# Attention: products of probabilities and values paired on TensorE's two column halves

## The chip, the cores and the metric

One core of one Trainium2 chip runs the whole layer. The metric is the device time of one execution in microseconds (us), the median of several runs. TensorE multiplies matrices (its weight loads are listed apart, as PEld), VectorE (DVE), ScalarE (ACT) and GpSimd (POOL) do the elementwise work, and SyncE (SP) issues the loads of the weights.

## The reference, cut to what matters

The layer is an encoder layer over 512 tokens of width 1024: a recurrent mixer and a windowed attention side by side, merged by gates, then a gated convolution network. Everything is float32. The change touches the attention alone. It has 8 query heads in two groups of four; the heads of a group share one head of keys and values (64 wide). The tokens are cut into four blocks of 128, and a query sees the keys of its own block and of the neighbours on either side, within 128 tokens:

```python
scores = jnp.einsum('bnqhgd,bnkhd->bnhgqk', qb, kb).astype(jnp.float32) * (hd ** -0.5)
...
probs = jax.nn.softmax(jnp.concatenate([scores, sink_logit], axis=-1), axis=-1)[..., :-1]
out = jnp.einsum('bnhgqk,bnkhd->bnqhgd', probs.astype(v.dtype), vb)
```

The last line is the product of probabilities and values. The first and the last block of queries see two blocks of keys, the two in the middle three, so there are ten pairs of a query block and a key block, for each of the two groups.

## The kernel before, in words

**The work around the attention.** Projections of the modulated input come first (`proj_tm`, `proj_fm`, names `tm` and `fm` in the profile). Each is a generator that yields after three matmuls with an estimate of their time. A class `Stream` holds a list of such projections, the background. `drive` (line 411) runs a foreground generator, and each number that the foreground yields is a time that is then filled with steps of the background. Thus the order of TensorE's instructions is laid out by the numbers `A0` to `A5` and their like (lines 34 to 51). An instruction that is passed through `kp` stays behind the instruction that was traced before it on its engine; others may be placed earlier by the scheduler, which works out the order of every engine from its own estimate of durations. When the background is used up, the branch product of the recurrent heads (`branch`, name `yr`, 96 matmuls) and the projections of the attention's gate (`use_ga`, line 956, name `fm` again, evicted by ScalarE at line 959) come after the attention in the program, and the scheduler puts them into the places where TensorE would wait.

**The attention** (from line 771). Eight units, one for each query block `tb` and group `kv`, in the order of `units`. `attention` (line 898) goes over them: in step `i` it runs `scores` of unit `i` and `values` of unit `i - 1` in turn, one step of either. Before the first group's unit of a block come `turn_k` and `turn_q`, which turn keys and queries (names `pk`, `pq`).

`scores` (line 814) multiplies for each of the four heads (name `as`), VectorE takes the product out of its bank with the running maximum (line 826), and after the fourth head come the statistics (lines 830 to 832 on VectorE), the exponentials (line 834 on ScalarE) and the normalization (line 840 on VectorE).

`values` (line 843) takes the normalized probabilities `s` of a unit. For each block of keys `b`, TensorE transposes four pieces of 128 x 128 (name `pt`, line 858), ScalarE evicts them into a tile `pT` of 128 x 512 (line 861), and after the next yield the inner function `product` (line 851) multiplies the block before with the values `v_att` (name `ao`, line 852). The product is float32, 64 rows of result by 512 columns, and goes to one half of the bank `outs[tb]`: to partitions 0 to 63 for the first group (`kv` 0), to 64 to 127 for the second, which is also the half of the array's columns that it uses. When the second group is done, ScalarE copies the bank into `o_att` (line 869).

**Banks and rings.** PSUM has three rings: `mm` (three banks, projections and branches), `sc` (two, transposes of probabilities and others) and `at` (three: scores, turned keys and queries, and the result `outs`). The tile `pT` has a ring of four. The recurrent scan uses the same way of halves as the change: `half_products` (line 595) multiplies float32 tiles of 64 columns in turn on the one and the other half of the array (names `pl`, `pd`, line 600).

Of the kernel before, what the change touches and what calls it, by code (L numbers as in the profile page):

```python
# [8 lines left out]
F32 = mybir.dt.float32  # L9
# [7 lines left out]
P = 128  # L17
# [6 lines left out]
HD = 64  # L24
# [7 lines left out]
C_AQ, C_AK, C_GR, C_GA = 2560, 3072, 3328, 4352  # L32
# schedule parameters
LEAD = 13600
# [10 lines left out]
A2 = 100  # L45
# [5 lines left out]
DVE0 = 6  # L51
# end of schedule parameters
TWO_PI = 6.283185307179586
# [8 lines left out]
def encoder_layer(  # L62
# [28 lines left out]

# [1 line left out]
    def w_tile():  # L93
# [21 lines left out]

# [1 line left out]
    ident = cn.tile([P, P], F32, name="ident")  # L117
# [6 lines left out]
    with tc.tile_pool(name="st", bufs=1) as st:  # L124
# [84 lines left out]

        # the first piece's last terms come from TensorE itself, which has nothing else to do yet  # L210
        first_pm = [sc_ps("pm0_0"), at_ps("pm0_1")]
# [107 lines left out]

# [1 line left out]
    # Each is a generator: TensorE's order is fixed, and what waits for other engines (scans, attention)  # L321
    # is placed between steps of projections that are ready.
    def load_cols(*cols):
# [29 lines left out]
    def proj_tm(use):  # L353
        def steps(parts):
            for b in range(2):
                acc = mm_ps(f"tm{b}")
                for i in range(2):
                    t = slice((2 * b + i) * P, (2 * b + i + 1) * P)
                    for k in range(KT):
                        hi, lo = parts[k // 4]  # L360
                        o = (k % 4) * 256
                        mm3(acc[:, i * 256:(i + 1) * 256], u_hi[:, k, t], u_lo[:, k, t], hi[:, o:o + 256],
                            lo[:, o:o + 256], k == 0, k == KT - 1, kp)
                        if i == 1 and k == KT - 1:
                            use(b, acc.rearrange("p (i n) -> p i n", i=2))
                        yield 327
        return steps
# [46 lines left out]

# [1 line left out]
    def ada_steps(col, done):  # L416
# [64 lines left out]

# [1 line left out]
    lbv = cols_a[:, 17:33].rearrange("p (d l h) -> p d l h", d=2, l=2)  # L483
# [23 lines left out]
    with tc.tile_pool(name="mx", bufs=1) as mx:  # L507
# [87 lines left out]
        def half_products(dst, keys, queries, other=0):  # L595
            # per block of 128: tokens of either half as keys, against the same half (or the other) as queries
            for cc in range(NTB):
                for a in range(2):
                    k_, q_ = cc * P + 64 * a, cc * P + 64 * (a ^ other)
                    kp(nc.tensor.matmul(dst[64 * a:64 * a + 64, q_:q_ + 64], lhsT=keys[:, k_:k_ + 64],  # L600
                                        rhs=queries[:, q_:q_ + 64], start=True, stop=True,
                                        tile_position=(0, 64 * a)))

        def scan_head(h, need):
# [21 lines left out]
            while L <= 128:  # L626
# [32 lines left out]
                L *= 2  # L659
            # across the blocks of 128: a running state per direction, the sum over past tokens of decayed k times v  # L660
            ktok = []
# [43 lines left out]
        def use_v(hh):  # L705
            return lambda b, a: nc.scalar.copy(v_rec[:, 2 * b:2 * b + 2, 256 * hh:256 * hh + 256], a)
# [18 lines left out]
        ri_load = lambda: ri_parts  # L725
        bg.add(ri_load, proj_tm(use_v(0)))                                                  # 1
        bg.add(load_cols(C_AK), proj_tm(use_kv))                                  # 2
        bg.add(load_cols(C_AQ), proj_tm(use_q(0)))                                # 3
        bg.add(load_cols(C_AQ + 256), proj_tm(use_q(1)))                          # 4
        for h in (2, 3):  # L730
            bg.add(load_cols(C_RFF + h * P, C_RFB + h * P), proj_fm(lambda f, a, h=h: gate_f(f, h, a)))
            bg.add(load_half(C_RQ + h * P), proj_fm(lambda f, a, h=h: silu_q(h, a), nf=1))
            if h == 2:
                bg.add(load_cols(C_RI + 256), proj_tm(use_v(1)))                  # 5 6 7, 8 9
        for hh in range(2):
            bg.add(load_cols(C_RG + 256 * hh), proj_tm(use_rg(hh)), ada_hook)               # 10 11
        gr_a = yin.tile([P, 2, S], F32, name="gr_a")
# [31 lines left out]

# [1 line left out]
        with tc.tile_pool(name="at", bufs=2) as at:  # L771
            units = [(tb, kv) for tb in range(NTB) for kv in range(2)]
            span = lambda tb: (max(tb - 1, 0), min(tb + 1, NTB - 1))
            probs, outs = {}, {}
            # scores of float32 accuracy in two passes: [hi; lo] of q on 128 rows against [hi; hi] and [lo; lo] of k
            kT = at.tile([P, 2, 2, S], F32R, name="kT", bufs=1)
# [65 lines left out]

            def values(tb, kv):
                lo_b, hi_b = span(tb)
                rw = slice(kv * HD, kv * HD + HD)
                s = probs.pop((tb, kv))
                if kv == 0:
                    outs[tb] = at_ps(f"ao{tb}")
                po = outs[tb]

                def product(b, pT):
                    kp(nc.tensor.matmul(po[rw, :], lhsT=v_att[:, b, rw], rhs=pT, start=(b == lo_b),
                                        stop=(b == hi_b), tile_position=(0, kv * HD)))
                last = None
                for b in range(lo_b, hi_b + 1):
                    pt = sc_ps(f"pt{tb}_{kv}_{b}")
                    for g in range(NG):
                        kp(nc.tensor.transpose(pt[:, g * P:(g + 1) * P],
                                               s[:, g, (b - lo_b) * P:(b - lo_b + 1) * P], ident))
                    pT = at.tile([P, 512], F32, tag="pT", name="pT", bufs=4)  # L860
                    nc.scalar.copy(pT, pt)
                    yield A2
                    if last is not None:
                        product(*last)
                    last = (b, pT)
                yield A2
                product(*last)
                if kv == 1:
                    nc.scalar.copy(o_att[:, :, tb * P:(tb + 1) * P], po.rearrange("p (g t) -> p g t", t=P))

# [3 lines left out]
            def rec_norm():  # L874
                # RMS norm and output gate of the recurrent heads
                nc.vector.tensor_scalar(rstat, rstat, 1.0 / P, RMS_EPS, ALU.mult, ALU.add)
                nc.scalar.activation(rstat, rstat, AF.Sqrt)
                nc.vector.reciprocal(rstat, rstat)
                for h in range(NH):
                    for tb in range(NTB):  # L880
                        nc.vector.scalar_tensor_tensor(out=o_tok[:, tb, h], in0=o_tok[:, tb, h],
                                                       scalar=rstat[:, tb, h:h + 1],
                                                       in1=rgs[:, tb, h * P:(h + 1) * P], op0=ALU.mult, op1=ALU.mult)
# [39 lines left out]

# [1 line left out]

# [27 lines left out]
    with tc.tile_pool(name="br", bufs=1) as br:  # L953
# [9 lines left out]
        def early_out():  # L963
            # the first two row blocks of w_out, into space that the recurrent branch has left
            hi = big.tile([P, 2, D], F32R, tag="x0", name="wo_hi")
            lo = big.tile([P, 2, D], F32R, tag="x1", name="wo_lo")
            raw = w_tile()
            rv = raw.rearrange("p (k n) -> p k n", n=D)
            nc.sync.dma_start(rv, w_out[0:2 * P, :].rearrange("(k p) n -> p k n", p=P))
            for k in range(2):  # L970
                nc.scalar.copy(hi[:, k], rv[:, k])
                nc.vector.tensor_tensor(out=lo[:, k], in0=rv[:, k], in1=hi[:, k].bitcast(F32), op=ALU.subtract)
                wo.append((hi[:, k], lo[:, k]))
# [48 lines left out]

# [1 line left out]
    u2p = ctx.enter_context(tc.tile_pool(name="u2p", bufs=1))  # L1024
# [129 lines left out]

# [1 line left out]
    ff = ctx.enter_context(tc.tile_pool(name="ff", bufs=2))  # L1156
# [37 lines left out]

# [1 line left out]
    vt = u2p.tile([P, 2, D], F32, tag="ua", name="vt")  # L1196
# [35 lines left out]
    for j in range(2):  # L1232
# [16 lines left out]
        for tb in range(NTB - j):  # L1249
# [3 lines left out]
            if j == 1:  # L1253
                mv = layer_stats(ff, bst2[:, tb, 0:2], f"b{tb}")
                for h in range(2):
                    scaled(tb, mv, 512 * h, 512 * h + 512)
                    store(tb, 512 * h, 512 * h + 512)
    # the last block ends in quarters
    tb = NTB - 1
# [37 lines left out]
```

## Time and profile before

| | |
|---|---|
| median of 3 runs | 826.77 us (825.41 to 827.01) |
| profiled execution, span from the first to the last instruction | 827.1 us; nothing of its time is recorded outside the span |
| TensorE matmuls busy | 803.9 us, 97% |
| VectorE busy | 577.4 us, 70% |
| ScalarE busy | 362.6 us, 44% |
| products of probabilities and values | 260.9 to 343.2 us |

Times inside the span are counted from its start. Matmuls are pipelined: the time that one takes from the stream is read from its start to the start of the next, not from its duration. A float32 matmul leaves two records.

### The profile page before, as it was taken

What the parts mean: (1) busy time and instruction counts of PE and PEld (TensorE: products, weight loads), DVE (VectorE), ACT (ScalarE), POOL (GpSimd) and SP (SyncE); (2) the same over time, 40 slices, a digit from 0 to 9 for tenths busy, and PEclk for the clock granted to TensorE, in tenths of its full rate; (3) what the DMA queues carried; (4) which work ended last, traced back from release to release, by engine and by line L of the source; (5) the groups of instructions that cost most, each with busy time, mean ns of one, the idle gap of its engine ahead of it and who ended that gap; (6) DMA issues with size and microseconds to landing.
All of it is one profiled execution on the core that took longest, in us unless ns stands there. A gap on an engine that the chain in (4) does not pass through costs nothing. (4 is left out here: it accounts for less than half of the span.)

```text
span 827.1 us, 11722 instructions
## 1 busy us (share of the span) xinstructions
PE 803.9 (97%) x4606; PEld 666.6 (81%) x4606; DVE 577.4 (70%) x959; ACT 362.6 (44%) x614; POOL 62.6 (8%) x88
## 2 busy tenths in 40 slices
PE   5999999999999999999999999999999999999996
PEld 4779998979887766688877888888888888888885
DVE  5869899597786656556788676787666678446537
ACT  3555555555374555633335354444444444221120
POOL 3431000000000000100154300000000000000000
PEclk9989999999999999999999999999999999999999
DMA  9964121322254403484640343456333323432202
GB/s 269 298 199 137 44 83 49 100 64 91 102 161 146 138 15 102 133 227 160 216 134 2 102 124 85 126 178 199 102 103 102 95 84 111 144 101 77 102 1 101
DMA packets 110727, 99.46 MB, mean 120 GB/s; under 512 B 3421, under 2 KB 98001, under 8 KB 110673
## 3 DMA queue, kind: packets, MB, share of 16 engines
q1 hardware_dynamic: 109024, 94.38, 37.8%
q0 software_dynamic: 1632, 4.33, 1.6%
q8 instruction: 36, 0.59, 0.3%
q14 instruction: 19, 0.15, 0.1%
q10 hardware_dynamic: 16, 0.00, 0.0%
HBM read 96.61 MB, written 2.10 MB: 119 GB/s over the span
## 5 line engine op out<-in xcount | busy, mean ns | idle before, releaser
L101 DVE TENSOR_TENSOR w_lo<-raw,w_hi 128x1024 fp32r<-128x1024 f32 x114 | 138.5, 1222 | 107.8 <-ACT w_hi L100 107.6
L100 ACT CAST w_hi<-raw 128x1024 fp32r<-128x1024 f32 x114 | 119.0, 1051 | 146.6 <-PE dn L108 76.2
L107 PE MATMUL up<-u_lo,w_hi 128*128 128x512 f32 (+1 forms) x384 | 143.5, 374 | 1.8 <-DVE u_lo L1119 1.8
L108 PE MATMUL up<-u_hi,w_lo 128*128 128x512 f32 (+1 forms) x384 | 143.4, 373 | 1.5 <-DVE w_lo L101 1.5
L106 PE MATMUL up<-u_hi,w_hi 128*128 128x512 f32 (+1 forms) x384 | 143.4, 374 | 0.0
L108 PEld LDWEIGHTS up<-u_hi,w_lo 128*128 128x128 f32 x384 | 73.1, 190 | 14.3 <-DVE w_lo L101 1.7
L107 PEld LDWEIGHTS up<-u_lo,w_hi 128*128 128x128 f32 x384 | 73.0, 190 | 14.3 <-DVE u_lo L1119 2.0
L106 PEld LDWEIGHTS up<-u_hi,w_hi 128*128 128x128 f32 x384 | 73.0, 190 | 12.5
L106 PE MATMUL fm<-u_hi,w_hi 128*128 128x512 f32 x176 | 72.8, 414 | 0.0
L106 PE MATMUL dn<-w_hi,g_hi 128*128 128x512 f32 (+1 forms) x198 | 72.6, 366 | 0.0
L107 PE MATMUL dn<-w_lo,g_hi 128*128 128x512 f32 (+1 forms) x198 | 72.5, 366 | 0.0
L108 PE MATMUL dn<-w_hi,g_lo 128*128 128x512 f32 (+1 forms) x198 | 72.4, 366 | 0.0
L108 PE MATMUL fm<-u_hi,w_lo 128*128 128x512 f32 x176 | 69.1, 393 | 0.0
L107 PE MATMUL fm<-u_lo,w_hi 128*128 128x512 f32 x176 | 68.9, 392 | 0.0
L106 PE MATMUL tm<-w_hi,u_hi 128*128 128x256 f32 x224 | 66.8, 298 | 0.0
L108 PE MATMUL tm<-w_hi,u_lo 128*128 128x256 f32 x224 | 63.2, 282 | 0.0
L107 PE MATMUL tm<-w_lo,u_hi 128*128 128x256 f32 x224 | 63.2, 282 | 0.0
L424 DVE SCALAR_TENSOR_TENSOR ada<-raw,silu_c,ada 128x1024 f32<-128x1024 f32 x32 | 41.0, 1282 | 9.3 <-DMA raw<-in_w_ada_dram 9.1
L106 PEld LDWEIGHTS tm<-w_hi,u_hi 128*128 128x128 f32 x224 | 42.7, 190 | 1.3
L107 PEld LDWEIGHTS tm<-w_lo,u_hi 128*128 128x128 f32 x224 | 42.9, 191 | 0.1
L108 PEld LDWEIGHTS tm<-w_hi,u_lo 128*128 128x128 f32 x224 | 42.7, 191 | 0.0
L106 PEld LDWEIGHTS dn<-w_hi,g_hi 128*128 128x128 f32 x198 | 37.4, 189 | 6.6 <-issue 0.4
(285 smaller groups left out, 1468.7 us busy)
## 6 DMA issues: line engine op xcount, KB each, us to landing
raw<-in_w_up_dram SPq DMA_DIRECT2D x44, 512.0 KB, 5.3
raw<-in_w_ada_dram SPq DMA_DIRECT2D x16, 1024.0 KB, 5.2
raw<-in_w_in_dram SPq DMA_DIRECT2D x15, 1024.0 KB, 5.1
raw<-in_w_down_dram SPq DMA_DIRECT2D x10, 1024.0 KB, 5.1
aw<-in_w_ada_dram SPq DMA_DIRECT2D x32, 256.0 KB, 5.4
raw<-in_w_out_dram SPq DMA_DIRECT2D x4, 1024.0 KB, 6.1
wq<-in_w_in_dram SPq DMA_DIRECT2D x24, 128.0 KB, 4.8
raw<-in_w_in_dram SPq DMA_DIRECT2D x6, 512.0 KB, 4.4
```

The costliest lines, as they stand in the source:

```text
L100: nc.scalar.copy(hi[:, 0:n], raw[:, o:o + n])
L101: nc.vector.tensor_tensor(out=lo[:, 0:n], in0=raw[:, o:o + n], in1=hi[:, 0:n].bitcast(F32), op=ALU.subtract)
L106: pin(nc.tensor.matmul(o, lhsT=sh, rhs=mh, start=start, stop=False))
L107: pin(nc.tensor.matmul(o, lhsT=sh, rhs=ml, start=False, stop=False))
L108: pin(nc.tensor.matmul(o, lhsT=sl, rhs=mh, start=False, stop=stop))
L424: nc.vector.scalar_tensor_tensor(out=acc, in0=raw[:, j * D:(j + 1) * D], scalar=silu_c[:, 2 * k2 + j:2 * k2 + j + 1], in1=acc, op0=ALU.mul ...
```

## The change

`values` no longer multiplies while it goes through the first group's unit. It keeps the transposed tiles of that unit in `turned[tb]`, one for each block of keys. In the second group's unit a new inner function `products` issues, for each block of keys, the product of the first group and that of the second one behind the other, to the two halves of the bank. The bank is taken when the first of them is issued. The ring of `pT` grows from four to seven. The first group's unit has one yield less. Comments elsewhere are left out, which changes no instruction.

```diff
-            probs, outs = {}, {}
+            probs, turned, outs = {}, {}, {}
...
                 s = probs.pop((tb, kv))
                 if kv == 0:
-                    outs[tb] = at_ps(f"ao{tb}")
-                po = outs[tb]
-
-                def product(b, pT):
-                    kp(nc.tensor.matmul(po[rw, :], lhsT=v_att[:, b, rw], rhs=pT, start=(b == lo_b),
-                                        stop=(b == hi_b), tile_position=(0, kv * HD)))
+                    turned[tb] = {}
+
+                def products(b, pT):
+                    if b == lo_b:
+                        outs[tb] = at_ps(f"ao{tb}")
+                    for v, p_ in ((0, turned[tb].pop(b)), (1, pT)):
+                        rw = slice(v * HD, v * HD + HD)
+                        kp(nc.tensor.matmul(outs[tb][rw, :], lhsT=v_att[:, b, rw], rhs=p_, start=(b == lo_b),
+                                            stop=(b == hi_b), tile_position=(0, v * HD)))
                 last = None
                 for b in range(lo_b, hi_b + 1):
...
-                    pT = at.tile([P, 512], F32, tag="pT", name="pT", bufs=4)
+                    pT = at.tile([P, 512], F32, tag="pT", name="pT", bufs=7)
                     nc.scalar.copy(pT, pt)
                     yield A2
-                    if last is not None:
-                        product(*last)
-                    last = (b, pT)
-                yield A2
-                product(*last)
+                    if kv == 0:
+                        turned[tb][b] = pT
+                    else:
+                        if last is not None:
+                            products(*last)
+                        last = (b, pT)
                 if kv == 1:
-                    nc.scalar.copy(o_att[:, :, tb * P:(tb + 1) * P], po.rearrange("p (g t) -> p g t", t=P))
+                    yield A2
+                    products(*last)
+                    nc.scalar.copy(o_att[:, :, tb * P:(tb + 1) * P],
+                                   outs.pop(tb).rearrange("p (g t) -> p g t", t=P))
```

## Rows read from the trace of the kernel before

**Rows 1.** The page: busy time of the engines, and busy tenths in 40 slices.

```profile
PE 803.9 (97%) x4606; PEld 666.6 (81%) x4606; DVE 577.4 (70%) x959; ACT 362.6 (44%) x614; POOL 62.6 (8%) x88
...
PE   5999999999999999999999999999999999999996
```

**Rows 2.** Stretches: busy us (instructions) by engine, then granted clock, DMA share, GB/s.

```profile
256.00:345.00 89.00, 88.89 (x403) 59.27 (x403) 53.42 (x146) 47.28 (x112) 2.11 (x5) 1.00 0.28 93
345.00:395.00 50.00, 50.00 (x249) 41.15 (x248) 32.16 (x35) 19.35 (x28) 2.07 (x4) 1.00 0.67 195
```

**Rows 3.** The tile of the products: duration ns min/median/max, first and last start.

```profile
L852 PE MATMUL ao<-pT,v_att x40: 592/592/643, 260.9 to 342.7; 128*64 128x512 f32 x40
```

**Rows 4.** Timeline of TensorE, a product among projections: start us, us, then the instruction.

```profile
260.55 0.40 PE L108 MATMUL fm<-u_hi,w_lo 128*128 128x512 f32 x1
260.87 1.07 PE L852 MATMUL ao<-pT,v_att 128*64 128x512 f32 x2
261.88 0.50 PE L106 MATMUL fm<-u_hi,w_hi 128*128 128x512 f32 x1
262.21 0.39 PE L107 MATMUL fm<-u_lo,w_hi 128*128 128x512 f32 x1
262.44 0.39 PE L108 MATMUL fm<-u_hi,w_lo 128*128 128x512 f32 x1
```

**Rows 5.** Timeline of TensorE, products among scores and transposes.

```profile
287.85 0.59 PE L824 MATMUL as<-kT,qT 128*128 128x384 f32 x2
288.28 0.60 PE L858 MATMUL pt<-ident,s 128*128 128x128 f32 x4
288.63 0.59 PE L824 MATMUL as<-kT,qT 128*128 128x384 f32 x2
289.15 1.07 PE L852 MATMUL ao<-pT,v_att 128*64 128x512 f32 x2
290.15 0.66 PE L858 MATMUL pt<-ident,s 128*128 128x128 f32 x4
290.56 0.59 PE L824 MATMUL as<-kT,qT 128*128 128x384 f32 x2
291.09 1.93 PE L852 MATMUL ao<-pT,v_att 128*64 128x512 f32 x4
292.95 0.66 PE L796 MATMUL pk<-ident,kk 128*128 128x128 f32 x4
...
312.92 1.93 PE L852 MATMUL ao<-pT,v_att 128*64 128x512 f32 x4
```

**Rows 6.** Timeline of TensorE, the recurrent scan's products on both halves.

```profile
83.99 0.69 PE L600 MATMUL pl<-qc,kc 128*64 128x64 f32 x16
84.60 0.39 PE L106 MATMUL tm<-w_hi,u_hi 128*128 128x256 f32 x1
```

**Rows 7.** Waits from 230 to 430 us: in total, times, longest.

```profile
PEld as L824 <- DVE stat L826: 1.8, 3, 0.8
```

**Rows 8.** Timeline, the last product and the first gate evictions; the tile of these.

```profile
342.17 1.07 PE L852 MATMUL ao<-pT,v_att 128*64 128x512 f32 x2
...
345.67 1.11 ACT L959 ACTIVATE ga<-fm 128x512 f32<-128x512 f32 x2
...
L959 ACT ACTIVATE ga<-fm x8: 591/598/620, 345.7 to 380.6; 128x512 f32<-128x512 f32 x8
```

**Rows 9.** Stretches for the tiles yr and fm alone; SP's timeline, gate weights.

```profile
273.00:343.50 70.50, 26.00 (x96) 17.45 (x96) 5.47 (x8) 1.00 0.28 92
...
326.50:343.50 17.00, 10.28 (x39) 7.05 (x39) 0.00 (x0) 0.00 (x0) 1.00 0.24 78
343.50:351.20 7.70, 6.50 (x28) 5.23 (x29) 0.00 (x0) 1.11 (x2) 1.00 0.56 171
...
282.98 3.27 SPq L329 DMA_DIRECT2D raw<-in_w_in_dram  x2
```

**Rows 10.** Timeline of VectorE: scores taken out, idle time before and its releaser.

```profile
304.28 0.56 DVE L826 CUSTOM_DVE_ANT_0 s<-as,band 128x384 f32<-128x384 f32 x1 [2.90 <-PE as L824]
```

More of the change, by code (lines that the diff above doesn't have):

```diff
@@ L844, in values @@
                 lo_b, hi_b = span(tb)
-                rw = slice(kv * HD, kv * HD + HD)
                 s = probs.pop((tb, kv))
                 if kv == 0:
-                    outs[tb] = at_ps(f"ao{tb}")
-                po = outs[tb]
-                def product(b, pT):
-                    kp(nc.tensor.matmul(po[rw, :], lhsT=v_att[:, b, rw], rhs=pT, start=(b == lo_b),
-                                        stop=(b == hi_b), tile_position=(0, kv * HD)))
+                    turned[tb] = {}
[6 more added lines that the diff above has]
+                                            stop=(b == hi_b), tile_position=(0, v * HD)))
                 last = None
```

## The prediction

> **What bounds the kernel now.** I read first the page's busy times and its 40 slices: TensorE is busy 97% of the span and 9 tenths or more in every slice between the first and the last [rows 1]. Then the table by stage: from 256 to 345 us, where the attention runs, TensorE is busy 88.89 of 89.00 us at a granted clock of 1.00 (the 2.4 GHz level), while VectorE has 53 and ScalarE 47 us of work; the next 50 us look the same [rows 2]. So in this stage the length of TensorE's own stream is the time, and what leaves that stream should leave the kernel, as long as other work stands ready to follow at once. Third, the tile of the products: 40 records, two for each of the 20 float32 products (ten blocks of keys times two groups of heads), each using 64 of the 128 columns of the array [rows 3].
>
> **What one product costs.** Alone between projections [rows 4]: from the projection that starts at 260.55 to the one at 262.21 are 1.66 us, and those hold two projection matmuls of 0.23 (262.21 to 262.44), so the product adds 1.66 - 0.46 = 1.20 us. Of this, 1.01 lie between its start and the next start; the other 0.19 are lost where the array goes from whole width to a half and back. Alone between scores and transposes [rows 5]: from 288.63 to 290.56 are 1.93 us with one pair of score matmuls (0.43, 287.85 to 288.28) and one group of four transposes (0.35), leaving 1.15. Two products in a row take 1.86 (291.09 to 292.95), so a second one directly behind costs 1.86 - 1.00 = 0.86. The 40 records stand in 18 bursts: two of four records (291.09 and 312.92), sixteen of two. With 1.18 for a burst (the middle of 1.15 and 1.20; both ends go into the range) the products cost 18 x 1.18 + 2 x 0.86 = 23.0 us now.
>
> **What a pair costs.** No 512-wide pair on both halves stands in the trace. The nearest row is the recurrent scan: there 8 float32 products of 64 columns alternate between the two halves, 16 records in one burst, and the next projection starts 0.61 us after the first of them [rows 6]. At the rate of one half (0.86 us for 512 columns, so 0.107 for 64), 8 products in turn would need 0.86 us beside the change of width; less the 0.14 that a lone burst has over its stream (1.00 - 0.86) there were 0.47, which is near four slots of 0.107. So there the two halves stream at the same time, each with its own moving operand and into the same bank, as in the new pairs. Bounds for a pair: a lone burst, 1.18 (nothing excludes full overlap, nothing could go below), and two in turn, 1.18 + 0.86 = 2.04. I take 1.19, the scan's row being the same kind of product. The sum: 10 x 1.19 = 11.9, so TensorE's stream shortens by 23.0 - 11.9 = **11.1 us** (10.8 to 11.3 with the ends of the burst's price).
>
> The Trainium skill ("TensorE: Matmul & The Clock Gate", Part 3) speaks against this: a weight load overlaps a running matmul only where the two use different row groups, and both halves of a pair use all rows. By that rule the pairs would run in turn and the sum would be 2.6 instead of 11.1; the scan's row does not bear it out.
>
> **The rest of the edit.** The 20 evictions of transposed probabilities and the 4 of results stay; ScalarE does the same work, nothing is issued to a DMA, SP's and POOL's queues keep their order in the program. The ring of transposed tiles goes from 4 to 7; three tiles wait through one unit and three more are made before they are read, so 7 are enough and no eviction waits. The accumulator is opened in the second group's half instead of the first's; the scores then have three banks instead of two for longer. Now the scores' weight loads stand 1.8 us behind VectorE's reading of such a bank [rows 7]; the gain on the chain lies between 0 and 1.8, nothing excludes either, and I take 0, since TensorE stayed busy meanwhile. One placing step is lost per first-group unit, so three background matmuls come a little later, at no cost while the background lasts. The new wait: each pair stands behind the second group's eviction of the block before, as the second group's products did; behind it in TensorE's fixed order stand the next transposes and scores. It stays covered as now.
>
> **What covers the saved time.** After about 273 us the background is used up, and TensorE's holes in the attention are filled with the branch product of the recurrent heads (96 matmuls, all used [rows 9]) and with projections of the attention's gate. The attention itself is a chain: scores, softmax on VectorE and ScalarE, transposes, next scores. Only products that stand before the last scores of a unit lengthen it. In the first group's units one product does, at 289.15 [rows 5] and in two more places alike (310.98, 332.17), 1.0 us each; in the first unit, among projections, both are in the way (2 x 1.20). So the chain ends 3.0 + 2.4 = 5.4 us earlier while TensorE has 11.1 less to do: 5.7 us, some 25 projections of 0.23, must be drawn forward. Is there enough? The accumulators of these projections are a ring of three banks, 3 x 24 = 72 matmuls. Their evictions write into space that the attention gives back, and they started only at 345.67, the first done 0.6 later, 3.1 us after the last product's end at 343.2 [rows 8]. By 343.5 the trace has 39 of them, by 351.2 another 28, so the 72nd, five more at 0.23, ends near 352.5 [rows 9]. The weights of the first two of their four loads were on the way by 286.3 [rows 9], and the space that their split waits for comes free by TensorE's own progress, so that it moves with it. Changed, the supply lasts to 352.5 - 11.1 = 341.4 and the first eviction is done at 343.2 - 5.4 + 3.1 = 340.9. The margin is 0.5 us: enough, barely. Where the chain is late by more, TensorE stands still for the excess. For the two-sided doubt in that margin (some microseconds either way, of which only one way costs) I set 0.6 us. Gain 11.1 - 0.6 = 10.5.
>
> The sum is made against the profiled execution, 827.1 us of span; the median of the runs shown, 826.77, is 0.3 below. 826.8 - 10.5 = **816.3 us**. A difference under 0.2%, 1.65 us, can't be told from none in this kernel.
>
> **Rivals.**
> 1. The cover tears (chance 0.15). Its place: VectorE's fixed order. In the trace the statistics of one unit stand behind the first scores of the next unit, for which VectorE waited 2.90 us, in turn for products that TensorE had first [rows 10]. One such wait more puts the end of the attention at 337.8 + 2.9 = 340.7, the first eviction at 343.8, and costs 343.8 - 341.4 = 2.4 us; gain 11.1 - 2.4 = 8.7, 818.1 us. Two cost 5.3: 821.0. For it: the program's order is worked out anew for the changed work. Against it: the change leaves fewer products between the scores.
> 2. The halves take turns (0.05): the change would not do what it says. Ten bursts of 2.04 are 20.4, gain 23.0 - 20.4 = 2.6, 824.2 us, and the shorter drawing forward needs no cover. Against it stands the scan's row. This is the case of the rule quoted above. Half overlap (one record of the pair hidden, half of 0.86 in ten pairs) would gain 6.8: 820.0, and has 0.05 of its own.
> 3. Slower (0.04): the same wait as in 1, in nearly every unit. From 273 us on there are six units; with five such waits, 14.5 us, the attention would end at 352.3, the first eviction at 355.4, TensorE would stand 14.0 us, and the time would be 826.8 - 11.1 + 14.0 = 829.7. It decides from an end of the attention near 351 on, that is 13 us later than in my sum. With three or four of them the result is no change (0.05).
> The forecast itself has 0.66, gain 9 to 11.5.
>
> **How the numbers follow.** The likeliest case gives 816.3. The range: its own lower end is 11.3 of gain plus half a microsecond for the reordering, 815.0; upward it takes in the cover torn twice and the half overlap, 821.5. Left out are the halves in turn, no change, slower, and something under 815, together near 0.18. Faster by over 0.2%: 0.66 + 0.15 + 0.05 + 0.05 = 0.91, of which I leave 0.02 to the middle because 824.2 lies near the edge: 0.89. Within 0.2%: 0.07. Slower: 0.04.
>
> **What the next profile would show.** Right: 40 product records in ten bursts of four, each a little over 1 us to the next start; TensorE busy nearly all of the stage; the end of the attention some 5 us earlier and all that follows some 10 us earlier, with the same distances. Wrong in the price: bursts of 1.8 us. Wrong in the cover: a hole in TensorE before the gate's fourth projection, with the evictions on ScalarE behind the attention's last product, or waits of VectorE for scores in more places than now. If neither shows and the time still falls by less than 9 us, the loss is after 345 us, in loads of weights that no longer keep ahead.

## The result and the profile after

| | before | after |
|---|---|---|
| median of 5 runs each | 826.79 us (825.41 to 829.37) | **815.0 us** (811.77 to 816.34) |
| ratio of the medians, 95% interval | | **0.9859** (0.9828 to 0.9890) |
| profiled execution: its own time, span | span 827.1 us | 811.77 us, span 810.0 us |
| last product of the attention starts | 342.7 us | 322.7 us |
| last projection of the attention's gate starts | 379.0 us | 363.4 us |

Forecast were 816.3 us in a range from 815.0 to 821.5; 815.0 us came, the lower edge of that range. The two profiled executions differ by 17.1 us, more than the medians' 11.8, so the first question is how much of that is the change's. After, the page still shows TensorE full:

```profile
PE 788.5 (97%) x4606; PEld 661.7 (82%) x4606; DVE 576.2 (71%) x959; ACT 363.0 (45%) x614; POOL 62.9 (8%) x88
...
PE   5999999999999999999999999999999999999996
```

To see what belongs to the change, one tile is followed that has projections on either side of the attention: `fm`. The tile's row gives the duration (ns, min/median/max) and the first and the last start. Before:

```profile
L106 PE MATMUL fm<-u_hi,w_hi x176: 387/389/501, 119.2 to 379.0; 128*128 128x512 f32 x176
```

And after, with the products' tile under it, which answers to [rows 3]:

```profile
L106 PE MATMUL fm<-u_hi,w_hi x176: 387/389/501, 114.3 to 363.4; 128*128 128x512 f32 x176
...
L856 PE MATMUL ao<-pT,v_att x40: 592/592/644, 267.7 to 322.7; 128*64 128x512 f32 x40
```

From the first to the last of these projections are 379.0 - 119.2 = 259.8 us before and 363.4 - 114.3 = 249.1 after: **10.7 us** less, in a stretch that holds the attention. The first start lies 4.9 us earlier, and from the last start to the end of the span are 448.1 us before and 446.6 after, 1.5 less; 10.7 + 4.9 + 1.5 = 17.1. These two remainders lie where TensorE's granted clock fell in the profiled execution of before and not in that of after. The stretches show it (columns as in [rows 2]). Before:

```profile
40.00:50.00 10.00, 7.91 (x29) 6.34 (x30) 10.00 (x21) 3.10 (x6) 2.93 (x2) 0.66 1.15 315
...
465.00:475.00 10.00, 8.22 (x57) 8.01 (x56) 5.82 (x6) 2.87 (x3) 2.87 (x3) 0.83 0.01 3
```

After, with the place that answers to the second of these, some 16 us earlier, and with the attention's two stretches, which answer to [rows 2]:

```profile
40.00:50.00 10.00, 9.73 (x57) 7.94 (x57) 9.24 (x19) 6.13 (x11) 3.52 (x3) 1.00 1.06 308
...
449.00:452.00 3.00, 1.21 (x10) 1.00 (x10) 2.96 (x3) 0.00 (x0) 2.71 (x3) 1.00 0.00 0
452.00:455.00 3.00, 3.00 (x28) 3.00 (x27) 0.55 (x1) 0.55 (x1) 0.39 (x1) 1.00 0.01 1
256.00:345.00 89.00, 89.00 (x471) 66.93 (x470) 60.27 (x149) 53.20 (x119) 3.54 (x6) 1.00 0.41 131
345.00:395.00 50.00, 50.00 (x249) 41.09 (x248) 34.83 (x45) 18.58 (x25) 1.62 (x3) 1.00 0.62 176
```

Granted clocks of 0.66 and 0.83 are means of the two levels: part of those 10 us ran at 1.2 GHz, each time after TensorE had stood for some 2 us (the 2.1 and 1.8 us that the busy times leave idle). After, TensorE stands as long at the second place, 1.8 us between 449 and 452 us, and the granted clock stays at 1.00. Neither place is near the change, and the experiments below show that the start comes at one time or another in either kernel. So 10.7 us is what the trace gives to the change, and the times, 11.8 us with an interval of 9.1 to 14.2, agree. The same distance, from the first to the last `fm`, is used for every run below: it is not moved by what the clock does at the start.

**The pair.** TensorE's timeline, at the place that answers to [rows 5]:

```profile
287.62 0.60 PE L824 MATMUL as<-kT,qT 128*128 128x384 f32 x2
288.15 1.08 PE L856 MATMUL ao<-pT,v_att 128*64 128x512 f32 x4
289.16 0.65 PE L862 MATMUL pt<-ident,s 128*128 128x128 f32 x4
289.57 0.60 PE L824 MATMUL as<-kT,qT 128*128 128x384 f32 x2
290.10 1.94 PE L856 MATMUL ao<-pT,v_att 128*64 128x512 f32 x8
291.97 0.62 PE L824 MATMUL as<-kT,qT 128*128 128x384 f32 x2
```

A pair, four records, takes 289.16 - 288.15 = 1.01 us to the next start, where a lone product, two records, took 1.00 in [rows 5]. From score to score are 289.57 - 287.62 = 1.95 us against 1.93 there: the second product of the pair costs nothing. Two pairs in a row take 1.87, so the second costs 0.86, as a second single product did.

**Where a pair is not free.** Two of the pairs wait inside:

```profile
267.69 1.64 PE L856 MATMUL ao<-pT,v_att 128*64 128x512 f32 x4
269.26 0.61 PE L824 MATMUL as<-kT,qT 128*128 128x384 f32 x2
...
320.99 2.29 PE L856 MATMUL ao<-pT,v_att 128*64 128x512 f32 x8
323.21 0.50 PE L446 MATMUL ga<-w_hi,ones_r 128*128 128x512 f32 x1
```

In the first there are 1.57 us to the next start instead of 1.01, 0.56 more; the second holds two pairs, 2.22 instead of 1.87. ScalarE's evictions of the second group's transposed probabilities, two in a row each time:

```profile
267.62 1.07 ACT L865 COPY pT<-pt 128x512 f32<-128x512 f32 x2
...
320.71 1.07 ACT L865 COPY pT<-pt 128x512 f32<-128x512 f32 x2 [2.14 <-PE pt L862]
```

One such copy takes 0.59 us, so the first of either two is done at 268.21 and 321.30, after the burst has started. From there to the next start are 1.05 us for the one pair and 1.91 for the two, about what pairs take that do not wait. So the second group's product stands behind the eviction: the first product's start shows only that its own operand is ready.

**The chain.** VectorE's waits for scores between 230 and 430 us (total, times, longest) before:

```profile
DVE s L826 <- PE as L824: 16.0, 16, 2.9
```

and after, with the wait that answers to [rows 7]:

```profile
DVE s L826 <- PE as L824: 10.1, 11, 1.6
PEld as L824 <- DVE stat L826: 1.6, 2, 0.8
```

The attention's last product, counted from the first `fm`, comes at 322.7 - 114.3 = 208.4 us, where it was at 342.7 - 119.2 = 223.5: **15.1 us** earlier. 5.4 were forecast. What covers TensorE at that point is seen in the gate's projections that stand ahead of the last product's end, and in their first eviction, which answers to [rows 8, 9]:

```profile
268.00:323.24 55.24, 5.50 (x22) 4.16 (x22) 0.00 (x0) 0.00 (x0) 1.00 0.25 79
...
L967 ACT ACTIVATE ga<-fm x8: 585/596/613, 325.9 to 365.0; 128x512 f32<-128x512 f32 x8
```

22 gate projections are drawn forward, where 39 were before [rows 9]: not more, as the prediction had it, but fewer.

### The profile page after: what moved, and what is told of

Its sections match the earlier page's. It is cut to its first block, busy times and chain, and to the rows that moved or that the text cites. A ratio compares the mean times of both kernels' runs of the same rounds, so it can differ in the third digit from the quotient of the medians.

```text
span 810.0 us, 11718 instructions
## 1 busy us (share of the span) xinstructions
PE 788.5 (97%) x4606; PEld 661.7 (82%) x4606; DVE 576.2 (71%) x959; ACT 363.0 (45%) x614; POOL 62.9 (8%) x88
## 5 line engine op out<-in xcount | busy, mean ns | idle before, releaser
L100 ACT CAST w_hi<-raw 128x1024 fp32r<-128x1024 f32 x114 | 119.0, 1051 | 145.7 <-PE dn L108 76.4
```

Source lines behind the costliest of these rows:

```text
L100: nc.scalar.copy(hi[:, 0:n], raw[:, o:o + n])
```

## The experiments

Two questions are put. First, what makes the gain: that the two halves stream at the same time (theory A), or that the products stand at another place (theory B)? Second, does the length of TensorE's stream set the time of the stage (again theory A), or does the chain of softmaxes (theory C)? The numbers of all runs, read as above: the distance from the first to the last `fm`, and that from the first `fm` to the last product.

Each ratio is taken to runs of the kernel before on the same chip.

| run | median us | ratio to before, 95% | first to last `fm` | first `fm` to last product |
|---|---|---|---|---|
| before | 826.79 | | 259.8 | 223.5 |
| after | 815.0 | 0.9859 (0.9828 to 0.9890) | 249.1 | 208.4 |
| e7_after, the same again | 814.42 | 0.9876 (0.9855 to 0.9897) | 249.1 | 208.4 |
| e1_apart | 828.85 | 1.0038 (1.0022 to 1.0054) | 264.2 | 229.0 |
| e2_in_turn | 816.69 | 0.9880 (0.9861 to 0.9898) | 250.3 | 208.9 |
| e3_alternate | 811.27 | 0.9819 (0.9804 to 0.9835) | 248.2 | 206.8 |
| e8_alternate, the same again | 812.7 | 0.9855 (0.9832 to 0.9878) | 248.2 | 206.8 |
| e4_ring | 824.36 | 0.9989 (0.9971 to 1.0007) | 259.9 | 223.5 |
| e5_chain2 | 815.29 | 0.9887 (0.9865 to 0.9908) | 249.0 | 213.9 |
| e9_chain4 | 824.47 | 0.9974 (0.9954 to 0.9994) | 258.0 | 222.9 |
| e6_chain8 | 836.59 | 1.0138 (1.0115 to 1.0162) | 270.9 | 235.3 |
| e10_bank_early | 815.64 | 0.9868 (0.9828 to 0.9907) | 249.1 | 208.4 |

The distances repeat to 0.1 us between runs of one kernel, while the first `fm` starts anywhere from 113.7 us (e7_after) to 119.0 (e10_bank_early) with the change, and without it at 119.2 (before) or 115.6 (e4_ring): so the 4.9 us at the start are no part of the change.

**e1_apart: the pairs taken apart.** The changed kernel, but the two products of a pair are issued at different places of the second group's unit, with transposes or a step of scores between them. In TensorE's order only one pair, in the last burst, is still made of neighbours.

```diff
+                    if kv == 1 and b == lo_b:
+                        product(0, b, turned[tb].pop(b))
...
+                    if kv == 1 and b > lo_b:
+                        product(0, b, turned[tb].pop(b))
...
-                            products(*last)
+                            product(1, *last)
```

Expected:

> The changed kernel with the products still made in the second group's unit, the ring of seven and the same yields, but the two products of a pair are kept apart: a group of transposes or scores stands between nearly all of them in TensorE's order (of the twenty, one pair of halves is still neighbours). Theory A (the gain is the two halves streaming at the same time): the products cost 15 bursts of 1.18 us and some seconds of 0.86, 21.5 us in place of the 11.8 that the changed kernel's bursts take, so about 9.7 us come back: 824 to 826 us, within 0.3% of the kernel before. Theory B (the gain is the later place of the products: a shorter chain, the bank held for less time): the gain stays, 814 to 817 us.

Measured 828.85 us, 0.38% over before: the gain is gone and some more. The stretch with the attention is 264.2 - 249.1 = 15.1 us longer than in the changed kernel. The products go back to their old price, as TensorE's timeline shows (two of one half, neighbours, take 1.86 again):

```profile
296.37 1.07 PE L855 MATMUL ao<-pT,v_att 128*64 128x512 f32 x2
297.37 0.62 PE L824 MATMUL as<-kT,qT 128*128 128x384 f32 x2
297.92 1.93 PE L855 MATMUL ao<-pT,v_att 128*64 128x512 f32 x4
299.78 0.62 PE L824 MATMUL as<-kT,qT 128*128 128x384 f32 x2
```

What is beyond that is a stall that the list of TensorE's waits shows, ahead of the last unit's transposes (the attention ends 20.6 us later than in the changed kernel, and all gate projections that can be drawn forward are used up, see e9), and a granted clock of 0.72 in the 6 us behind it:

```profile
PE pt L863 <- DVE s L840: 3.0, 1, 3.0
```

```profile
340.00:346.00 6.00, 5.71 (x17) 2.54 (x18) 2.16 (x5) 2.66 (x4) 0.31 (x1) 0.72 0.26 104
```

At 0.72 some 56% of those 6 us ran at 1.2 GHz, 3.4 us that did the work of 1.7; 15.1 - 3.0 - 1.7 = 10.4 us are left for the pairing. Counted by bursts, with the prediction's prices and the 0.9 us of waits seen above, the products take 16 x 1.18 + 3 x 0.86 = 21.46 us here and 7 x 1.18 + 3 x 0.86 + 0.9 = 11.74 in the changed kernel, 9.7 more; the other 0.7 is not told apart. Theory A.

**e2_in_turn and e3_alternate: order of the same products at one place.** All products of a block of queries at the end of the second group's unit; A is a product of the first group, B of the second. In e2 the order is A A B B (A A A B B B with three blocks of keys), in e3 A B A B.

```diff
-                    for v, b in [(v, b) for v in range(2) for b in range(lo_b, hi_b + 1)]:
+                    for v, b in [(v, b) for b in range(lo_b, hi_b + 1) for v in range(2)]:
```

(minus e2, plus e3). Expected of e2:

> All products of a block of queries in one burst at the end of the second group's unit: first all of the first group, then all of the second, so that neighbours in TensorE's order use the same half, but for one place where the group changes. Theory A, TensorE starting its matmuls in order: bursts of 3 slots of 0.43 x 2 = 0.86 us for the blocks with two keys and of 5 for those with three, that is 4 x 1.18 + 12 x 0.86 = 15.0 us, 3.2 more than the changed kernel: about 818 us. Theory A with each half working through a queue of its own: 2 and 3 slots, 9.9 us, about 813. Theory B: no difference from the next kernel, whatever both are.

and of e3:

> The same single burst at the end of the unit, but in the order first group, second group, first, second: neighbours use different halves. Theory A: 2 slots for blocks with two keys, 3 for those with three, 4 x 1.18 + 6 x 0.86 = 9.9 us, 1.9 less than the changed kernel and 5.1 less than the burst in turn: about 813 us. Theory B: equal to the burst in turn.

A burst of two blocks of keys and one of three in TensorE's timeline, e2:

```profile
269.08 2.15 PE L855 MATMUL ao<-pT,v_att 128*64 128x512 f32 x8
271.15 0.62 PE L824 MATMUL as<-kT,qT 128*128 128x384 f32 x2
...
306.63 3.70 PE L855 MATMUL ao<-pT,v_att 128*64 128x512 f32 x12
310.26 0.50 PE L824 MATMUL as<-kT,qT 128*128 128x256 f32 x2
```

and e3:

```profile
267.59 2.15 PE L855 MATMUL ao<-pT,v_att 128*64 128x512 f32 x8
269.67 0.62 PE L824 MATMUL as<-kT,qT 128*128 128x384 f32 x2
...
304.19 2.79 PE L855 MATMUL ao<-pT,v_att 128*64 128x512 f32 x12
306.92 0.50 PE L824 MATMUL as<-kT,qT 128*128 128x256 f32 x2
```

With three blocks it is 3.63 us against 2.73 for the same six products. Three slots of 0.86 and the 0.14 of a burst are 2.72: e3 has full overlap. e2 needs a fourth slot, 3.58, and no fifth or sixth. With two blocks both orders take the same, 2.07 us in e2 (269.08 to 271.15) and 2.08 in e3 (267.59 to 269.67). (The last block's bursts wait for an eviction in both and take 2.50 (from 322.26) and 2.22 (from 318.93).) So B runs beside A even where one more product of A's half is queued between them, and with two between them it comes one slot late. That was in none of the expected cases. The four bursts together take 11.8 us in e2 and 9.8 in e3, and the stretches differ by the same 250.3 - 248.2 = 2.1: at one place, the order alone makes this difference. Against the changed kernel e2 is 1.2 us longer and e3 0.9 shorter.

**e8_alternate and e7_after: e3 and the changed kernel again, side by side.**

> The version with all products of a block at the end of the second group's unit, the two halves in turn (the run called e3_alternate), again, beside the changed kernel on one chip. Theory A (halves that alternate stream together, a longer burst has the same price per pair and one change of width less): 1 to 3 us under the changed kernel. If the earlier difference came from the runs alone: the two agree within 0.2%.

> The changed kernel itself, on the same chip as the two with the longer chain. Theory A and C alike: 815 within 2 us, ratio to the kernel before 0.983 to 0.989.

812.7 us against 814.42: 1.7 us, with intervals that overlap. The trace repeats to 0.1 us: 248.2 against 249.1. So e3 beats both kernels, in this stretch by 0.9 us over the changed one; the times alone could not have shown that.

**e4_ring: the kernel before with the larger ring alone.**

```diff
-                    pT = at.tile([P, 512], F32, tag="pT", name="pT", bufs=4)
+                    pT = at.tile([P, 512], F32, tag="pT", name="pT", bufs=7)
```

> The kernel before with the ring of transposed tiles grown from four to seven and nothing else. Theories A and B both: no change, within 0.2% of the kernel before. If the larger ring had let the evictions run ahead, up to 2 us less.

0.9989 with an interval that holds 1; the stretch is 259.9 us against 259.8. The ring by itself does nothing.

**e5_chain2 and e6_chain8: a longer chain, the same stream.** Copies of the scores onto themselves on ScalarE, which change no value, two or eight in a unit (`n` here):

```diff
+                for g in range(n):
+                    nc.scalar.copy(s[:, g % NG, 0:nk], s[:, g % NG, 0:nk])
                 nc.scalar.activation(e_, e_, AF.Exp)
```

Expected of e5:

> The changed kernel with two more copies on ScalarE in each unit of the attention, of scores onto themselves, between the exponentials and the normalization; no value changes. They make every unit's chain about 1.1 us longer, so the attention ends 6 to 8 us later. Theory A (TensorE's stream bounds the stage; in the changed kernel the work drawn forward outlasts the first gate eviction by about 10.4 us, so the chain may end that much later at no cost): the time stays, 815 within 1.7 us, and TensorE's idle time in the attention stays under 0.5 us. Theory C (the gain comes from the shorter chain of softmaxes, not from the shorter stream): what lengthens the chain comes back in the time, 6 to 8 us, 821 to 823.

and of e6:

> The same with eight such copies in each unit, some 4 us or a little more per unit, so that the attention ends 26 to 31 us later. Theory A: the cover of about 10.4 us is used up and TensorE stands still for the excess, 16 to 21 us, ahead of the gate's fourth projection, whose bank waits for ScalarE's first eviction: 830 to 836. Theory C: the whole lengthening comes back, 841 to 846. If the scheduler finds other work to place there, or the chain is lengthened by less because other idle time absorbs the copies, the time is lower in both, and the idle time of TensorE against the delay of the first gate eviction tells them apart: the difference of the two is about 10 us under A and near 0 under C.

e5: the last product comes 213.9 - 208.4 = 5.5 us later and the time is 815.29 us, beside 814.42 of the changed kernel on that chip; the stretch is 0.1 us shorter. So the chain does not set the time, and theory C, by which those 5.5 us should have come back, falls. The rows of the stretch and, for `fm` alone, of what stands ahead of the last products:

```profile
256.00:345.00 89.00, 89.00 (x474) 67.68 (x473) 60.85 (x153) 56.43 (x133) 3.48 (x6) 1.00 0.37 120
```

```profile
272.00:329.20 57.20, 11.73 (x47) 8.87 (x47) 0.00 (x0) 0.00 (x0) 1.00 0.26 80
```

TensorE stays full, by drawing 47 gate projections forward instead of 22. e6 takes 836.59 us, just over the 830 to 836 of theory A and under the 841 of theory C: the last product comes 26.9 us later and the stretch grows by 21.8, so 5.1 us are taken by cover. That is neither the 10 of theory A's expectation nor near 0; and TensorE stood elsewhere than expected, ahead of transposes:

```profile
PE pt L864 <- DVE s L842: 15.3, 3, 6.5
```

The row of `fm` says why: all 48 projections of two accumulators have started by 321.6 us (what the second stretch shows is the end of the last), and the third accumulator's come only behind the attention's end.

```profile
272.00:321.60 49.60, 11.72 (x48) 8.94 (x48) 0.00 (x0) 0.00 (x0) 1.00 0.33 101
321.60:353.80 32.20, 0.13 (x1) 0.00 (x0) 0.00 (x0) 0.00 (x0) 0.69 0.23 74
```

**e9_chain4: how much cover there is.** The same with four copies.

> The changed kernel with four such copies per unit on ScalarE, which should end the attention 10 to 12 us later (two copies ended it 5.5 us later). It asks how much work really stands ahead of the attention's end as cover. If three accumulators, 72 gate projections, can be drawn forward, as the prediction had it, the margin of the changed kernel is 10.4 us and the time rises by at most 2: 814 to 816.5. If TensorE's fixed order holds only the first two accumulators, 48 projections, ahead of the attention's last product, the cover is the 26 of them that follow that product in the changed kernel, 26 x 0.23 = 6.0 us; TensorE then stands for the other 4 to 6 us, and more if its clock falls with it: 818.5 to 823, with the idle time in the holes ahead of transposes, not ahead of the gate's fourth tile.

824.47 us, a little over the second case's range. TensorE's timeline and the stretches around it:

```profile
327.96 0.71 PE L824 MATMUL as<-kT,qT 128*128 128x256 f32 x4
336.10 2.03 PE L864 MATMUL pt<-ident,s 128*128 128x128 f32 x8 [7.43 <-ACT w_hi L100]
338.06 2.55 PE L858 MATMUL ao<-pT,v_att 128*64 128x512 f32 x8
340.54 0.50 PE L446 MATMUL ga<-w_hi,ones_r 128*128 128x512 f32 x1
```

```profile
326.00:330.00 4.00, 2.67 (x18) 1.89 (x16) 4.00 (x12) 3.45 (x5) 0.00 (x0) 1.00 0.13 14
330.00:334.00 4.00, 0.00 (x0) 0.00 (x0) 1.79 (x5) 2.23 (x9) 0.00 (x0) 0.81 0.99 312
334.00:338.00 4.00, 1.90 (x8) 1.48 (x8) 2.62 (x7) 2.68 (x7) 0.00 (x0) 0.50 0.51 199
```

TensorE has nothing left and stands 7.43 us until the last unit's probabilities are normalized, which VectorE does from 335.60 on (the releaser that the row names, a cast on ScalarE, only ended at about that time):

```profile
335.60 1.14 DVE L842 TENSOR_SCALAR s<-s,stat 128x256 f32<-128x256 f32 x4
```

Then the transposes run at a granted clock of 0.50: eight of them last 338.06 - 336.10 = 1.96 us, where four took 0.35 in [rows 5]; part of this is the normalization, which goes on until 336.74. The last product comes 14.5 us later and the stretch grows by 8.9, so 5.6 us were covered: the 26 projections, 6.0 us, that stood behind the last product in the changed kernel, and not 72.

**e10_bank_early: the accumulator opened in the first group's unit**, as before the change; every engine's order stays that of the changed kernel.

```diff
                 if kv == 0:
                     turned[tb] = {}
+                    outs[tb] = at_ps(f"ao{tb}")
...
-                    if b == lo_b:
-                        outs[tb] = at_ps(f"ao{tb}")
```

> The changed kernel with the accumulator of the products opened in the first group's unit, as before the change, so that the scores have two banks instead of three meanwhile; all engines' orders of instructions stay those of the changed kernel. It asks why the attention ended 15.1 us earlier (net of the start) where 5.4 were forecast. If the third bank shortened the waits between scores and softmax: the attention ends 4 to 10 us later than in the changed kernel, and VectorE's waits for scores rise from 10.1 us towards 16; the time stays within 1.7 us, since 6 us of cover are left. If the new order of the instructions did it: the attention's end moves by less than 2 us, and the time stays.

Nothing moves: both distances are those of the changed kernel to 0.1 us, and so are VectorE's waits for scores:

```profile
DVE s L826 <- PE as L824: 10.1, 11, 1.6
```

So the third bank is not what shortened the chain. What is left, by elimination, is the new order of the instructions; which part of it was not tried.

## Why the prediction was right, and where it was not

- **A pair costs what a lone product costs: right.** 1.01 us to the next start where 1.00 was taken, from the scan's 64-wide products to the 512-wide pair. e1 gives the same from the other side, 10.4 us back when the pairs are parted. The rule of the Trainium skill ("TensorE: Matmul & The Clock Gate", Part 3) that a weight load overlaps a running matmul only with other row groups would, as the prediction took it, have made the pair 1.86 us; here both halves use all rows and it took 1.01, so the measurement decides against it for column halves. The Trainium skill says elsewhere ("TensorEngine Tiling (Array Packing)", Tiling Modes) that tiles operate independently and load and multiply in parallel; with that the runs agree where the halves alternate (1.01 us for a pair, 2.73 for three).
- **The stream shortens by 11.1 us: right by 0.4, through two misses that cancel.** The sum had ten bursts of 1.19, 11.9 us. The trace has seven bursts, since in three places two pairs stand in a row, which saves 3 x (1.19 - 0.86) = 1.0; and two waits inside pairs cost 0.56 + 0.35 = 0.9. That these are nearly equal is luck. The step "It stays covered as now" for the wait on the second group's eviction was wrong at these two places. The stretch shortened by 10.7; the 0.4 is not told apart.
- **"The chain ends 5.4 us earlier": wrong, 15.1.** The products that leave the path were counted; the order that the scheduler lays out anew was not. As TensorE is busy throughout, the 15.1 us are what no longer stands ahead of the last product: the 10.7 us of the stretch, 39 - 22 = 17 projections (3.9 us) and two matmuls of `ga` (some 0.5). The forecast had 25 more projections drawn forward, so the chain left 42 x 0.23 = 9.7 us less to fill than it expected, and that is 15.1 - 5.4. VectorE's waits for scores fell from 16.0 to 10.1 us, and e10 shows that the accumulator's bank, which the prediction set at 0 to 1.8 and took as 0, gives indeed nothing. Rival 1 and rival 3 expected the new order to add waits; it removed some. What else shortened the chain is not told apart.
- **"3 x 24 = 72" projections as cover: wrong, 48.** The third accumulator's projections were not drawn ahead of the attention's end in any run: in TensorE's order they stand behind the last steps of a modulation vector, `ga` and `adac`, and those stand about the last product (in e9 `ga` follows it at 340.54). The trace of before had it too: its 39 projections by 343.5 [rows 9] lie within two accumulators. The ring's size was read as the supply. Whether another order could bring the third one forward was not tried.
- **The margin of 0.5 us, and the 0.6 set aside for it: right in its effect only.** Both errors bear on it with opposite signs. With 48 and an end 5.4 us earlier, 25 more than 39 would have had to be drawn forward, 16 more than there are: 16 x 0.23 = 3.7 us of stall, 826.8 - 11.1 + 3.7 = 819.4 us, and more where the clock falls after it, as in e9. With the end 15.1 us earlier, 17 fewer were drawn forward and 6.0 us of cover were left over. So the likeliest case came, for a reason that the working did not have.
- **TensorE's stream bounds the stage: right.** e5 makes the chain 5.5 us longer and the time stays; e9 and e6 give where that ends.
- **Nothing after 345 us comes in the way: right.** The stretch from 345 to 395 us is busy 50.00 of 50.00, and the last `fm` carries the whole 10.7 us.
- **The rivals.** Rival 1, the torn cover, did not come: TensorE is busy for all of the 89 us, and what waits it has in the attention are the 0.9 us inside two pairs. Rivals 2 and 3 have no trace in the result either: no burst of 1.8 us for a single pair, and the attention ended earlier, not later.

The median is 1.3 us under the forecast. 0.6 us of this are what was set aside for the margin; the rest is less than the interval of the medians (9.1 to 14.2 us of gain) can resolve, so that 815.0 fell on the edge of the range and not beyond it is luck.

## What to carry to other kernels

Here a product on half of the columns took 1.00 us alone, and two on different halves 1.01 together: put them next to each other, in turn (A B A B), with both operands ready, and the second one is free. Where TensorE is full, the gain is what leaves its stream, as long as other ready work fills the holes: count that work from what TensorE's order really holds ahead of the critical result, not from the number of banks. And when an edit lets a scheduler order the work anew, the forecast of the other engines' waits is open in both directions.

## What the runs showed of the hardware that was not expected

- Six products A A A B B B on two halves take four slots (3.63 us), A B A B A B three (2.73), and A A B B two (2.07), as many as A B A B. So a product of the idle half ran ahead of one that waited for the busy half, and not ahead of two; longer queues were not tried.
- A stall can cost more than its length. In e9 TensorE stood 7.43 us; behind it the granted clock was 0.50 from 334 to 338 us, and the stretch grew by 8.9 us in all. In e1 3.0 us of standing were followed by a granted clock of 0.72 over 6 us, 1.7 us more. Not every stall costs this: after one of 1.8 us the granted clock fell in the profiled execution of before and stayed at 1.00 in that of after.
